# A macaron decoder trunk on one core: seven-product groups put in a set order

## The chip, the core and the metric

The kernel runs on one core of a Trainium2 chip, in one launch. The metric is the device time of that launch in microseconds (us); the program on the core has five engines: TensorE (PE, matmuls), VectorE (DVE), ScalarE (ACT), GpSimd (POOL) and SyncE (SP, which issues the loads).

## What is computed

The input is x (512 tokens, width 1024) and a conditioning vector c. Two layers; each has three sub-layers, with shift, scale and gate made from c:

```python
cs = jax.nn.silu(c)
for l in range(DEPTH):                                   # 2
    mod = (cs @ ada_w[l] + ada_b[l]).reshape(B, N_SUB, 3, D_MODEL)[:, :, :, None, :]
    h = _rmsnorm(x, norm_g[l, 0]) * (1.0 + mod[:, 0, 1]) + mod[:, 0, 0]
    x = x + 0.5 * mod[:, 0, 2] * _swiglu(h, ffn_w_gate[l, 0], ffn_w_up[l, 0], ffn_w_down[l, 0])
    h = _rmsnorm(x, norm_g[l, 1]) * (1.0 + mod[:, 1, 1]) + mod[:, 1, 0]
    x = x + mod[:, 1, 2] * _mixer(h, w_in[l], conv_w[l], w_conv_out[l], w_attn_out[l], w_o[l], rel_bias)
    h = _rmsnorm(x, norm_g[l, 2]) * (1.0 + mod[:, 2, 1]) + mod[:, 2, 0]
    x = x + 0.5 * mod[:, 2, 2] * _swiglu(h, ffn_w_gate[l, 1], ffn_w_up[l, 1], ffn_w_down[l, 1])
return _rmsnorm(x, final_g)
# _swiglu(h, wg, wu, wd) = (silu(h @ wg) * (h @ wu)) @ wd, hidden width 2816
```

The change touches only the gate and up products of `_swiglu`, of which there are four in the program.

## The kernel before

All is float32. Activations stand transposed: `hh` and `hl` hold the sub-layer's input h as a high part (rounded to the matmul's input form) and a low part (the rest), 8 chunks of 128 rows by 512 tokens. Each weight tile is split in the same way: ScalarE casts the high part, VectorE subtracts it for the low part. A product is then three matmuls: high by high, high by low, low by high. Weights are loaded by SyncE into four buffers `raw` of 1 MB; split parts stand in slots of 512 columns, 49 in `R`; float32 scratch in 19 slots `F`. There are eight PSUM banks in three rotations: `mm` (4), `at` (2), `o` (2).

**A feed-forward** (`ffn`, L618) has 22 hidden tiles of 128 rows. The first two (three in the first feed-forward of the program) get their gate and up sums in the stage ahead, `boundary`, and are handed over as `first`, standing in PSUM banks; in the first feed-forward tile 3 is made plainly (16 chunk steps of three matmuls for gate and up). All others are made in pairs by a scheme with seven block products in place of eight (`seven`, L537). With gate weights a (first four chunks) and c (last four), up weights b and d, and h cut in quarters, a pair of tiles needs

- product 1: a by the first chunks of the first half of the tokens, and product 2: c by the last chunks of that half. They need no sum.
- product 5: (b - a) by sum 1; product 6: (d - (b - a)) by sum 2; product 7: (d - b) by sum 3; product 3: d by sum 4. Each needs a block sum of h.
- product 4: (c - (d - b + a)) by the last chunks of the second half.

A product (`product`, L518) is 24 matmuls of 256 columns; it needs a cast of 128x1024 on ScalarE and a low part of 128x1024 on VectorE. Differences of weights are made by VectorE in place in `raw` (L558). Results gather in three banks: `one` (in `mm`, products 1, 6, 7, 4, with copies by ScalarE between them, L554), `two` (in `at`, product 2) and `three` (in `o`, products 5 and 3). VectorE adds the copies and banks (`plus`, L561). `swiglu_pair` then takes the silu of the gates, multiplies, and splits the result into the slots that `down` reads.

**Order.** `ffn` begins with `Sums` (L488): all four block sums of h (VectorE, 128x1024 each, in the float32 copy `whole`, 8 slots of `F`) and their splits, into the upper 16 slots of `R`; `whole` is given back at once. Then the hidden tiles come in five parts (L44: 0 to 6, 6 to 12, 12 to 16, 16 to 19, 19 to 22), most followed by `down`, which multiplies that part's activations with the down weights and adds to x. Within `up` (L664) a group runs 5, 6, 2, 7, then product 1 of the next group (`begin`), then 4, 3, and then its `swiglu_pair`. The text's order is a priority: a planner lays out each engine's instructions from it ahead of time, and may take a later one first where it expects the earlier one not to be ready. On the chip each engine follows the laid-out order.

**Beside it** run, in the first feed-forward and the mixers, modulation steps (L297: load 512 KB of ada weights, multiply and sum on VectorE, 1024 columns). `tick` (L152), called twice a product and every second plain step, lets so many of them through as rate and share allow.

`boundary` (L452) ends the stage before: the last three chunks of its down product, the norm, the modulated h, and the first hidden tiles' sums, in two halves of 256 tokens.

## Time and profile before

| | us |
|---|---|
| median of 3 runs | 2684.92 (2683.99 to 2691.61) |
| the profiled execution | 2685.69 |
| its span on the core | 2683.9 |
| TensorE busy | 2620.5 |
| VectorE busy | 1838.3 |
| ScalarE busy | 1171.6 |

The four feed-forwards start, in the profiled execution, at about 67, 1034, 1391 and 2341 us; between them lie the start of the program (0 to 67), the first mixer (390 to 1010) and the second (1719 to 2318). A matmul counts as busy from its start to the modelled end of its pipeline, so matmuls of 256 columns 0.12 us apart show 0.28 us each. Where a row merges several instructions, x24 is their count. "idle" or a figure in brackets is the time in which the engine did nothing before that instruction, with what ended it.

### The profile page before, as it was taken

How to read it: one execution, taken by the hardware profiler on the slowest of the kernel's cores; microseconds unless marked ns; L12 is line 12 of the kernel's file. 1: busy time of each engine (PE TensorE's matmuls, PEld its weight loads, DVE VectorE, ACT ScalarE, POOL GpSimd, SP SyncE). 2: the span in 40 equal slices, each digit the busy share in tenths (PEclk: the TensorE clock that was granted, in tenths of full speed). 3: DMA queues.
4: the chain of work that ended last, by engine and by line, in shares of the span. 5: the costliest groups of instructions: out<-in, count | busy, mean ns of one | idle time of the engine just before them, and what ended most of it. 6: DMA issues, size and time to landing. Idle time of an engine off the chain costs nothing.

```text
span 2683.9 us, 40526 instructions
## 1 busy us (share of the span) xinstructions
PE 2620.5 (98%) x16265; PEld 2347.2 (87%) x16265; DVE 1838.3 (68%) x2874; ACT 1171.6 (44%) x2200; POOL 227.7 (8%) x551
## 2 busy tenths in 40 slices
PE   6899999999999999999999999999999999999999
PEld 5798999788888889989999999988888888989998
DVE  7996778888463358667787777885536534677675
ACT  4453454343353236434554444543443423544443
POOL 1000023121010001000020000330110000200001
PEclk8999999999999999999999999999999999999999
DMA  8732246767222231333224332562322322133321
GB/s 282 249 128 91 93 146 222 270 203 248 75 95 79 87 118 44 99 110 109 96 64 130 106 110 77 179 217 86 97 69 79 118 81 85 63 111 99 98 83 67
DMA packets 285480, 326.42 MB, mean 122 GB/s; under 512 B 8057, under 2 KB 263404, under 8 KB 285292
## 3 DMA queue, kind: packets, MB, share of 16 engines
q1 hardware_dynamic: 284836, 323.19, 36.8%
q8 instruction: 127, 2.08, 0.3%
q10 hardware_dynamic: 456, 0.65, 0.1%
q14 instruction: 61, 0.50, 0.1%
HBM read 321.67 MB, written 2.13 MB: 121 GB/s over the span
## 4 chain that ended last, share of the span: by engine, by line
PE 84%; DVE 9%; DMA 3%; ACT 3%; issue 1%; POOL 1%; DVEq 0%; POOLq 0%; SPq 0%; ACTq 0%
PE mm L531 16%; PE mm L234 12%; PE mm L235 12%; PE mm L236 12%; PE o L531 8%; PE at L531 4%; PE mm L1046 3%; DMA slots_f<-in_ada_t_dram 2%; DVE slots_f L297 2%; PE o L234 2%; PE o L236 2%; PE o L235 2%; PE at L236 2%; PE at L234 2%; PE at L235 2%; DVE slots_r L145 2%
## 5 line engine op out<-in xcount | busy, mean ns | idle before, releaser
L214 DVE TENSOR_TENSOR slots_r<-raw,slots_r 128x512 fp32r<-128x512 f32 (+2 forms) x578 | 361.0, 642 | 340.5 <-PE mm L235 162.1
L213 ACT CAST slots_r<-raw 128x512 fp32r<-128x512 f32 (+2 forms) x584 | 325.1, 582 | 403.2 <-PE mm L236 170.9
L234 PE MATMUL mm<-hh,slots_r 128*128 128x512 f32 (+1 forms) x1320 | 487.8, 370 | 0.0
L235 PE MATMUL mm<-hl,slots_r 128*128 128x512 f32 (+1 forms) x1320 | 483.0, 366 | 0.0
L236 PE MATMUL mm<-hh,slots_r 128*128 128x512 f32 (+1 forms) x1320 | 482.2, 365 | 0.0
L145 DVE TENSOR_TENSOR slots_r<-raw,slots_r 128x1024 fp32r<-128x1024 f32 (+3 forms) x401 | 379.9, 970 | 130.2 <-ACT slots_r L522 55.4
L522 ACT CAST slots_r<-raw 128x1024 fp32r<-128x1024 f32 x273 | 282.5, 1048 | 363.0 <-DVE raw L558 93.7
L236 PEld LDWEIGHTS mm<-hh,slots_r 128*128 128x128 f32 x1320 | 248.4, 188 | 43.3
L234 PEld LDWEIGHTS mm<-hh,slots_r 128*128 128x128 f32 x1320 | 248.9, 189 | 36.5
L235 PEld LDWEIGHTS mm<-hl,slots_r 128*128 128x128 f32 x1320 | 248.9, 189 | 36.1
L531 PE MATMUL mm<-slots_r 128*128 128x256 f32 x1872 | 240.6, 284 | 3.5 <-ACT slots_r L522 2.2
L531 PE MATMUL o<-slots_r 128*128 128x256 f32 x1872 | 236.3, 283 | 5.1 <-DVE slots_r L145 5.0
L531 PEld LDWEIGHTS o<-slots_r 128*128 128x128 f32 x1872 | 229.9, 191 | 8.1 <-DVE slots_r L145 6.2
L531 PEld LDWEIGHTS mm<-slots_r 128*128 128x128 f32 x1872 | 230.8, 191 | 6.4 <-ACT slots_r L522 2.8
L531 PE MATMUL mm<-hh,slots_r 128*128 128x256 f32 x1248 | 229.5, 280 | 2.7 <-DVE slots_r L145 1.3
L234 PE MATMUL mm<-slots_r 128*128 128x512 f32 (+1 forms) x584 | 212.3, 364 | 0.2 <-ACT slots_r L649 0.2
L235 PE MATMUL mm<-slots_r 128*128 128x512 f32 (+1 forms) x584 | 212.3, 364 | 0.0
L236 PE MATMUL mm<-slots_r 128*128 128x512 f32 (+1 forms) x584 | 212.1, 363 | 0.0
L297 DVE CUSTOM_DVE_ANT_0 slots_f<-slots_f 128x1024 f32<-128x1024 f32 x144 | 176.1, 1232 | 42.0 <-DMA slots_f<-in_ada_t_dram 41.0
L531 PEld LDWEIGHTS mm<-hh,slots_r 128*128 128x128 f32 x1248 | 193.7, 188 | 5.7 <-DVE slots_r L145 2.2
L558 DVE TENSOR_TENSOR raw<-raw 128x1024 f32<-128x1024 f32 x156 | 189.6, 1220 | 2.2
L531 PE MATMUL mm<-hl,slots_r 128*128 128x256 f32 x624 | 174.0, 279 | 0.0
(194 smaller groups left out, 4373.7 us busy)
## 6 DMA issues: line engine op xcount, KB each, us to landing
slots_f<-in_ada_t_dram SPq DMA_DIRECT2D x144, 512.0 KB, 4.5
raw<-in_w_in_dram SPq DMA_DIRECT2D x52, 1024.0 KB, 5.7
raw<-in_ffn_w_gate_dram SPq DMA_DIRECT2D x42, 1024.0 KB, 5.3
raw<-in_ffn_w_up_dram SPq DMA_DIRECT2D x42, 1024.0 KB, 6.2
raw<-in_ffn_w_down_dram SPq DMA_DIRECT2D x32, 768.0 KB, 4.3
raw<-in_w_in_dram SPq DMA_DIRECT2D x48, 512.0 KB, 5.3
raw<-in_ffn_w_down_dram SPq DMA_DIRECT2D x20, 512.0 KB, 3.5
raw<-in_w_conv_out_dram SPq DMA_DIRECT2D x8, 1024.0 KB, 4.8
```

Of the source, the lines that this page charges most:

```text
L145: V.tensor_tensor(out_, a, b, op=ALU.subtract)
L213: A.copy(hv, src)
L214: (eng or V).tensor_tensor(lv, src, f(hv), op=ALU.subtract)
L234: T.matmul(dst, hi, xh[:, cols], start=first, stop=False)
L235: T.matmul(dst, hi, xl[:, cols], start=False, stop=False)
L236: T.matmul(dst, lo, xh[:, cols], start=False, stop=last)
L297: V.tensor_tensor_reduce(out=w, in0=w, in1=cs.ap, scale=1.0, scalar=0.0, op0=ALU.mult, op1=ALU.add, accum_out=m[:, k:k + 1])
L522: A.copy(hv, src)
L531: T.matmul(dst, a, b, start=first and k == i == n == 0, stop=True, skip_group_check=True)
L558: V.tensor_tensor(dst, x, y, op=ALU.subtract)
L1046: T.matmul(dst, a, b, start=k == 0 and r % 2 == 0 and n == 0, stop=True, skip_group_check=True)
```

## The change

- `Sums` no longer makes all sums at once: `make(i)` makes and splits one, and is called from the first group's run: sums 1 and 2 about product 6, sum 3 ahead of product 7, sum 4 ahead of products 4 and 3. `whole` is given back after the first group.
- `product` and `seven` become classes whose splitting and running are separate calls.
- The first group (`first_group`) splits products 1, 2 and 5 ahead of everything else in `ffn`, product 5 into the place of sum 4 (`room`); its loads are asked for there. It keeps its bank `one` in `o` instead of `mm`.
- Ahead of the parts come the swiglus of `first` (odd count) and the plain tile, then products 1 and 2 of the first group.
- A group in `up` runs 5, 6, then 1 of the next group, 7, then 2 of the next group, then 4, 3. Splits 5 and 6 stand first; `swiglu_pair` of the group before stands behind them, or at the end of the part.
- After the last group `R.top` is raised, so that later takers may use all of `R`.

```diff
     class Sums:
+        def make(self, i, whole):
             h11, h21 = whole[:, :4, HALF[0]], whole[:, :4, HALF[1]]
             h12, h22 = whole[:, 4:, HALF[0]], whole[:, 4:, HALF[1]]
-            V.tensor_tensor(h22, h21, h22, op=ALU.add)
-            self.split(0, h22)
-            V.tensor_tensor(h21, h11, h21, op=ALU.subtract)
-            V.tensor_tensor(h22, h22, h11, op=ALU.subtract)
-            self.split(1, h22)
-            self.split(2, h21)
-            V.tensor_tensor(h22, h12, h22, op=ALU.subtract)
-            self.split(3, h22)
+            dst, a, b, op = ((h22, h21, h22, ALU.add), (h22, h22, h11, ALU.subtract),
+                             (h21, h11, h21, ALU.subtract), (h22, h12, h22, ALU.subtract))[i - 1]
+            V.tensor_tensor(dst, a, b, op=op)
+            hi, lo = (v[:, i - 1] for v in self.parts)
+            A.copy(hi, dst)
+            sub(lo, dst, f(hi))
+        def room(self):
+            return [v[:, 3].rearrange("p k n -> p (k n)") for v in self.parts]
...
+    class Seven:
+        def __init__(self, raw1, raw2, sums, tag="mm"):
+            self.a, self.c = raw1[:, :4], raw1[:, 4:]
+            self.b, self.d = raw2[:, :4], raw2[:, 4:]
+            self.sums = sums
+            self.one, self.two, self.three = bank(tag), bank("at"), None
...
+        def run1(self):
+            self.p1.run()
+            self.c11 = self.kept(self.one)
+        def run2(self):
+            self.p2.run()
+            self.plus(self.c11, self.two)
+        def split5(self, room=None):
+            self.minus(self.a, self.b, self.a)
+            self.three = bank("o")
+            self.p5 = Product(self.a, self.sums(1), self.three, True, room)
+        def split6(self):
+            self.minus(self.a, self.d, self.a)
+            self.p6 = Product(self.a, self.sums(2), self.one)
+        def run56(self):
+            self.p5.run()
+            self.p6.run()
+            self.c12 = self.kept(self.one)
...
+        def run43(self):
+            self.p4.run()
+            self.p3.run()
+            self.plus(self.c12, self.three)
+    def first_group(raws):
+        sums = Sums()
+        group = Seven(*raws, sums, "o")
+        group.split1()
+        group.split2()
+        group.split5(sums.room())
+        return group
...
     def ffn(l, i, get, first, whole):
         acts = {}
         R.top = N_LOW
-        sums = Sums(whole.ap.rearrange("p (k n) -> p k n", k=NC))
-        whole.give()
+        group = first_group(get.raws(len(first) + len(first) % 2))
...
+        modulating["share"] = SHARE_UP
+        if len(first) % 2:
+            for n, banks in enumerate(first):
+                swiglu(n, *banks)
+            banks = [any_bank() for _ in range(2)]
+            for pd, u in zip(banks, get(len(first))):
+                project([(pd, u)], h, NC)
+            swiglu(len(first), *banks)
+        group.run1()
+        group.run2()
...
         def up(part):
             modulating["share"] = SHARE_UP
+            late = None
             for m in range(*part):
-                if m in acts:
+                if m not in groups:
                     continue
...
-                pair = ahead.pop(m)
-                next(pair)
-                begin(m + 2)
-                for _ in pair:
-                    pass
-                if m + 2 == DFF // P:
+                here, after = groups.pop(m), None
+                if not begun[0]:
+                    make(1)
+                    here.split6()
+                    make(2)
+                    if len(first) % 2 == 0:
+                        for n, banks in enumerate(first):
+                            swiglu(n, *banks)
+                else:
+                    here.split5()
+                    here.split6()
+                    if late:
+                        swiglu_pair(*late)
+                if m + 2 < DFF // P:
+                    after = groups[m + 2] = Seven(*get.raws(m + 2), sums)
+                    after.split1()
+                here.run56()
+                make(3)
+                here.split7()
+                if after:
+                    after.run1()
+                    after.split2()
+                here.run7()
+                here.split43()
+                make(4)
+                if after:
+                    after.run2()
+                here.run43()
+                if not begun[0]:
+                    begun[0] = True
+                    whole.give()
+                late = m, *here.out()
+                if not after:
                     sums.give()
+                    R.top = N_R
+            if late:
+                swiglu_pair(*late)
```

## Rows read from the trace of the kernel before

**Rows 1.** Busy time of TensorE on the page: us, share of span, instructions
```profile
PE 2620.5 (98%) x16265; PEld 2347.2 (87%) x16265; DVE 1838.3 (68%) x2874; ACT 1171.6 (44%) x2200; POOL 227.7 (8%) x551
```

**Rows 2.** Stretches: busy us and (instructions) of PE, PEld, DVE, ACT, POOL; clock; DMA; GB/s
```profile
390.00:1034.00 644.00, 631.23 (x3425) 540.76 (x3424) 420.36 (x780) 263.23 (x604) 96.24 (x243) 1.00 0.44 146
1034.00:1075.00 41.00, 36.68 (x300) 35.48 (x299) 35.86 (x37) 24.50 (x33) 0.00 (x0) 1.00 0.22 71
...
1391.00:1402.00 11.00, 8.76 (x69) 8.15 (x68) 10.86 (x13) 7.98 (x11) 0.00 (x0) 1.00 0.00 0
1402.00:1719.00 317.00, 317.00 (x2243) 298.15 (x2242) 233.64 (x307) 146.87 (x230) 11.84 (x18) 1.00 0.36 114
...
2341.00:2366.00 25.00, 20.47 (x152) 19.43 (x151) 21.21 (x22) 15.02 (x19) 0.00 (x0) 0.93 0.26 84
...
2352.00:2357.00 5.00, 4.62 (x26) 4.62 (x27) 4.91 (x5) 0.33 (x1) 0.00 (x0) 0.66 0.02 5
```

**Rows 3.** TensorE's waits at A, B, C, D: releaser, us in all, times, longest
```profile
PE at L236 <- DVE slots_r L214: 6.8, 1, 6.8
...
PE o L531 <- DVE slots_r L145: 3.3, 1, 3.3
...
PE mm L531 <- ACT slots_f L627: 1.1, 1, 1.1
...
PE mm L531 <- ACT slots_r L522: 1.7, 1, 1.7
```

**Rows 4.** TensorE in order of time (start, us), and one product from the chain
```profile
68.30 0.39 PE L234 MATMUL mm<-hh,slots_r 128*128 128x512 f32 x1
...
111.28 0.40 PE L234 MATMUL mm<-slots_r 128*128 128x512 f32 x1
...
1034.40 0.39 PE L531 MATMUL o<-slots_r 128*128 128x256 f32 x1
...
1040.20 0.28 PE L531 MATMUL at<-hh,slots_r 128*128 128x256 f32 x1
1043.75 2.90 PE L531 MATMUL o<-slots_r 128*128 128x256 f32 x22 [3.28 <-DVE slots_r L145]
...
1316.62 2.88 PE mm L531 x24
```

**Rows 5.** VectorE in order of time: start, us, what it made, wait ahead of it
```profile
64.50 2.29 DVE L1282 TENSOR_TENSOR slots_f<-hh,hl 128x2048 f32<-128x2048 f32 x1
...
80.46 0.69 DVE L214 TENSOR_TENSOR slots_r<-raw,slots_r 128x512 fp32r<-128x512 f32 x1
...
105.07 1.22 DVE L145 TENSOR_TENSOR slots_r<-raw,slots_r 128x1024 fp32r<-128x1024 f32 x1
...
1023.45 1.23 DVE L495 TENSOR_TENSOR slots_f<-slots_f 128x1024 f32<-128x1024 f32 x1
...
1028.65 2.36 DVE L145 TENSOR_TENSOR slots_r<-raw,slots_r 128x1024 fp32r<-128x1024 f32 x2 [2.71 <-ACT slots_r L522]
...
1042.48 1.22 DVE L145 TENSOR_TENSOR slots_r<-raw,slots_r 128x1024 fp32r<-128x1024 f32 x1
...
1061.43 1.22 DVE L145 TENSOR_TENSOR slots_r<-raw,slots_r 128x1024 fp32r<-128x1024 f32 x1
1062.57 0.68 DVE L561 TENSOR_TENSOR slots_f<-slots_f,o 128x512 f32<-128x512 f32 x1
...
2330.91 1.22 DVE L495 TENSOR_TENSOR slots_f<-slots_f 128x1024 f32<-128x1024 f32 x1
```

**Rows 6.** Groups by line and shape, 67 to 112; the cast from 1023 to 1075
```profile
L297 DVE CUSTOM_DVE_ANT_0 slots_f<-slots_f 128x1024 f32<-128x1024 f32 x9 | 10.9, 1216 | 0.0
...
L145 DVE TENSOR_TENSOR slots_r<-slots_f,slots_r 128x512 fp32r<-128x512 f32 x4 | 2.7, 686 | 0.6 <-ACT slots_r L630 0.6
L561 DVE TENSOR_TENSOR slots_f<-slots_f,o 128x512 f32<-128x512 f32 x2 | 1.4, 688 | 0.2 <-PE o L531 0.2
...
L522 ACT CAST slots_r<-raw 128x1024 fp32r<-128x1024 f32 x15 | 15.2, 1048 | 10.4 <-DVE raw L558 6.5 <-PE o L531 2.1 <-PE mm L531 1.2
```

More of the change, by code (lines that the diff above doesn't have):

```diff
@@ L537, in seven, with __init__, run @@
-    def seven(raw1, raw2, sums, done):
-        a, c = raw1[:, :4], raw1[:, 4:]
-        b, d = raw2[:, :4], raw2[:, 4:]
-        def run(*args):
-            p = product(*args)
-            next(p)
-            return p
-        def end(p):
-            for _ in p:
-                pass
-        def kept(src):
+    class Product:
+        def __init__(self, src, x, bank_, first=False, room=None):
+            self.x, self.bank, self.first = x, bank_, first
+            self.slots = [] if room else [R.take(2), R.take(2)]
+            self.parts = [a.rearrange("p (k m) -> p k m", k=4) for a in room or (s.ap for s in self.slots)]
+            hv, lv = self.parts
+            A.copy(hv, src)
+            sub(lv, src, f(hv))
+        def run(self):
+            hv, lv = self.parts
+            for k in range(4):
+                xh, xl = self.x(k)
+                for i in range(2):
+                    c_ = slice(i * P, (i + 1) * P)
+                    dst = self.bank[:, HALF[i]]
+                    for n, (a, b) in enumerate(((hv[:, k, c_], xh), (hv[:, k, c_], xl), (lv[:, k, c_], xh))):
+                        T.matmul(dst, a, b, start=self.first and k == i == n == 0, stop=True, skip_group_check=True)
+                if k % 2:
+                    tick()
+            for s in self.slots:
+                s.give()
@@ L572, in seven, with split1 @@
-        end(run(a, sums(2), one))
-        u2 = kept(one)
-        two = bank("at")
-        end(run(c, quarter(1, 0), two, True))
-        plus(p1, two)
-        minus(b, d, b)
-        end(run(b, sums(3), one))
-        u3 = kept(one)
-        plus(u3, three)
-        yield
-        minus(c, c, a)
-        end(run(c, quarter(1, 1), one))
-        end(run(d, sums(4), three))
-        plus(u2, three)
-        done(p1, u2, one, u3)
+        def split1(self):
+            self.p1 = Product(self.a, quarter(0, 0), self.one, True)
@@ new lines, in ffn @@
+        wv = whole.ap.rearrange("p (k n) -> p k n", k=NC)
+        sums = group.sums
+        modulating["share"] = SHARE_UP
[8 more added lines that the diff above has]
+        group.run2()
+        groups = {len(first) + len(first) % 2: group}
```

114 lines of the change are left out of this document (43 added, 71 removed).

## The prediction

> **What bounds the kernel now.** I read the page's busy shares first: TensorE is busy 98% of the span [rows 1]. So time can only come from TensorE's own stops or from its clock, as the change removes no matmul. Next the busy time by stretch [rows 2], cut at the four feed-forward starts (I call them A, B, C, D). Between 1402 and 1719, the rest of C with its nine later groups, TensorE is never idle: in the steady run of groups there is nothing to win. All that this change can reach lies just behind the boundaries: 74 to 82 (A), 1034 to 1075 (B), 1391 to 1402 (C), 2341 to 2366 (D). The waits of TensorE there [rows 3] say who ended the stops: a low part from VectorE, a high part or a drained bank from ScalarE. There are 1, 3, 3 and 5 such stops (of each stretch one row stands). Last, the order on the two engines around them [rows 4, 5]: in B the product on bank `o` (product 5) waits 3.28 us for its low part, made at 1042.48, while VectorE, busy 35.9 of the 41 us of B [rows 2], worked on block sums and on the first SwiGLUs. In A the low part of a plain unit comes at 80.46, behind all four sums. So the stops are made by order where VectorE has room, and by its load where it has none. Which is it, for each start?
>
> **VectorE's load up to the last product of the first group.** With the change TensorE runs 1, 2, 5, 6, 1', 7, 2', 4, 3 (a dash marks the next group): nine products at 2.88 us [rows 4]. Before product 3 can start, VectorE must make nine low parts, four raw differences, four sums and four low parts of sums: 21 operations of 128x1024. Two of them back to back take 2.36 us where one takes 1.22 [rows 5, 6], so one each 1.14 us: 23.9 us. Two plus operations and the multiply and low part of each swiglu of the `first` list come on top, at 0.69 us [rows 6].
> B, C and D (no modulations, two swiglus): 23.9 + 6 x 0.69 = 28.0 us. In B VectorE is free at 1023.45 and waits 2.71 us for a slot that the boundary still reads [rows 5]; it would be done at 1023.45 + 2.7 + 28.0 = 1054.2. TensorE, leaving the boundary at 1034.4, comes to product 3 at 1034.4 + 8 x 2.88 = 1057.4 [rows 4]. Slack 3.2 us: order alone can remove these stops. In D VectorE is free at 2330.91 [rows 5] and TensorE at about 2341: 2361.6 against 2364.0, slack 2.4 us. For C I take the same.
> A is different: four swiglus, two plain-unit splits and the modulation steps of its ticks are queued too. The check is the trace itself: VectorE is free at 66.8 (64.50 + 2.29) and ends the last low part of the first group at 106.29 [rows 5], seven modulation steps of 1.2 us among it (nine take 10.9 [rows 6]). The change asks for the same plus one low part (2'), so 107.4; product 3 would end at 107.4 + 2.88 = 110.3. Before, eight products ended at 111.28 [rows 4] and the ninth (2 of the next group) was still to come: 114.2 on the same footing. Gain 3.9 us, not the 6.8 us of the stop. If the planner let every modulation go behind, TensorE would set the end: 68.30 + 48 x 0.23 + 9 x 2.88 = 105.3, gain 8.9; if more modulations came ahead, nothing.
>
> **The change part by part.**
> - Sums at their products, room for product 5 in the fourth sum's place, splits 1, 2 and 5 first: no operation more or less, only order. Takes away in B 41.0 - 36.7 = 4.3 us of idle, in C 11.0 - 8.8 = 2.2, in D 25.0 - 20.5 = 4.5 [rows 2]. The cover is TensorE's own products 1 and 2, which need no sum: 5.8 us in which VectorE makes four operations (4.6 us).
> - Clock: after D's stops 26 matmuls ran between 2352 and 2357 at a mean granted clock of 0.66, part of it at 1.2 GHz, part at 2.4; they took 4.6 us where 26 x 0.12 = 3.1 us is what they take at 2.4 GHz [rows 2]. Gone with the stops: 1.5 us. (In A the clock fell as well, but there VectorE sets the end.)
> - Restart: the 3.28 us stop of B lies between matmul starts 3.55 us apart, against 0.12 within a product: 3.43 lost, 0.15 more than the row says [rows 4]. Eleven stops in B, C and D: 1.7 us.
> - Product 2 a group ahead: one product more per feed-forward runs before the first `down`, one less behind it; within the steady run it is exchanged for product 1', between 6 and 7. The bank `one` is still copied out behind another product each time (1' covers the copy after 6, 2' that after 7). Cost nothing as long as VectorE and ScalarE keep ahead (1402 to 1719: VectorE 234 of 317 us, ScalarE 147 [rows 2]); uncovered it is a copy a group, the third rival's kind of price.
> - Swiglu behind the next splits: its multiplies and low parts (4 x 0.69 on VectorE) move behind two splits; at a part's end it stands ahead of `down` as it did. Who waits: `down` reads the last two activations only at the end of its first jobs, as before. Nothing.
> - Loads: weights of the next group are asked for earlier in the text, past no other load, but the four raw buffers come free by the same last splits of the group before, so the two SyncE issues leave when they did. The eight slots of the whole h are given back later, and the modulation loads of A queue for what is left; bound 0 to one late step (1.2 us), taken 0.
> - New wait: the first group's `one` now stands in a bank `o`, as `three` does, and there are two. Product 5 of the second group, directly behind product 3, needs one of them: it waits for the plus that reads `three` (0.69 us and the drain of the last matmul, 0.28) unless `one` was read by then. Behind it on TensorE stand 6' and all else. In A `down` comes between. Three times 0 to 0.97; I take 0.9, nearest to the plus's own row [rows 6]: 2.7 us lost. Between these two groups the trace of before has no such wait, as `one` was in one of four banks `mm`. The Trainium skill (Perfetto Trace Analysis, Optimization Strategy) says that the same gap coming back can mean that there is not enough PSUM for the next tile; by that rule it would come back at each group, but from the second group on `one` is in `mm` again, so I charge it once a feed-forward.
> - The free slots after the last group (`R.top` raised) change which slots the boundary takes; it can make C like B and D, whose sums share slots with the boundary's units: inside C's slack. Taken as 0, bounds -1 to +1.
>
> Sum: 3.9 + 4.3 + 2.2 + 4.5 + 1.5 + 1.7 - 2.7 = 15.4 us. The profiled execution took 2685.69 us (span 2683.9, 1.8 around it); the median of the three is 2684.92, 0.77 less. 2685.7 - 15.4 - 0.8 = 2669.5 us.
>
> **Rivals.**
> 1. The load, not the order (2684 us). If the slots of the sums are read by the boundary's matmuls to its end, VectorE can begin only at about 1034.4 + 2.3 (a cast and a low part): 1036.7 + 28.0 = 1064.7 against TensorE's 1057.4, so some 7 us of stops, no less than now. It decides from a start 3.2 us later than I assumed. Then B, C and D win nothing and A's 3.9 pays for the banks: -1.2 us. For it: the 2.71 us that VectorE waited there. Against it: behind that wait it made the low parts of two products at 1028.65, well ahead of the boundary's end [rows 5].
> 2. The border of groups (2693 us, slower). Plus of `three` waits for product 3; if the next group's differences and low parts are queued behind it, TensorE stands for 0.69 + 1.22 + 1.05 + 1.22 = 4.2 us (the 1.05 is the cast on ScalarE [rows 6]). There are 23 borders inside the parts; from 0.67 us each on average it eats the whole gain, and every fourth border at 4.2 us costs 24 us. For it: the text of the change puts splits 5 and 6 behind run43, and the steady run has no other cover there. Against: before, the text stood the same way and the trace has the next low part (1061.43) ahead of the plus (1062.57) [rows 5]: the planner put first what was ready first. The Trainium skill (TensorE: Matmul & The Clock Gate, Architectural detail) says that VectorE and ScalarE take their instructions strictly in order, and matmuls stay in program order; by that rule nothing on the chip mends a bad order at a border, and the 80.46 row, a ready split that was late, agrees.
> 3. The change does not do what it says (2685 us). The order on the engines is the planner's; in B the sum-free products already run first. If it keeps its order, nothing changes.
>
> **How the numbers follow.** Forecast 0.60, rival 1 0.20, rival 2 0.15, rival 3 0.05. About 0.3% (8 us) is what a measurement of this kernel can tell from no change: faster below 2677, slower above 2693. Faster 0.60 (the forecast), same 0.24 (rivals 1 and 3 without a remnant), slower 0.16. The low end: A's 8.9 in place of 3.9, no bank waits (2.7) make 2661.8; the rest of the kernel is planned anew too, and its stops (first mixer, 12.8 us between 390 and 1034 [rows 2]) may move by half: 2655. The high end takes in rivals 1 and 3 and the lighter half of rival 2: 2691. Left out are the heavier half of rival 2 and a gain beyond all counted stops.
>
> **What would show it.** Right: no wait of TensorE over 1 us behind the boundary in B and D, and the granted clock at 1.00 there; the first low parts on VectorE are those of 1, 2 and 5, with the sums behind; in A stops of some 5 us are left, late in the group, ended by VectorE; one wait of under 1 us ahead of product 5 of the second group. Wrong: idle of TensorE at borders, ended by VectorE's plus or ScalarE's cast, or a stretch like 1402 to 1719 with idle in it; or A gaining nothing, which would mean that VectorE's load there is larger than counted.

## The result, and the profile after

The changed kernel takes 2674.38 us (median of 5 runs, 2671.10 to 2678.67). The kernel before, run beside it, has the median 2684.92 (5 runs, 2683.99 to 2691.61). The ratio of the two, formed from the runs beside each other, is 0.9948 with a 95% interval of 0.9935 to 0.9960: faster by 0.5%. The forecast was 2669.5 us. The profiled execution of the changed kernel took 2671.10 us (span 2669.3) against 2685.69 (2683.9) before: 14.6 us less, where the sum said 15.4. That single execution is the fastest of its five, so the agreement of these two numbers is closer than what the medians show (10.5 us apart); it is the split of the 14.6 that teaches something, and it isn't the split that was forecast.

The page of the changed kernel, the line that answers to [rows 1]:

```profile
PE 2617.5 (98%) x16265; PEld 2346.9 (88%) x16265; DVE 1832.5 (69%) x2874; ACT 1171.1 (44%) x2200; POOL 232.9 (9%) x551
```

The same instructions on every engine, so only order has changed. The stretches, with the columns of [rows 2] (length, busy us and instructions of PE, PEld, DVE, ACT, POOL; granted clock; DMA share; GB/s):

```profile
390.00:1031.00 641.00, 629.23 (x3404) 540.14 (x3403) 423.45 (x780) 263.42 (x604) 95.80 (x239) 0.99 0.45 147
1031.00:1076.00 45.00, 45.00 (x381) 45.00 (x380) 41.49 (x48) 29.31 (x42) 0.00 (x0) 1.00 0.31 100
1388.00:1402.00 14.00, 14.00 (x118) 13.92 (x118) 13.96 (x15) 6.59 (x10) 0.00 (x0) 1.00 0.23 77
1402.00:1709.00 307.00, 303.96 (x2121) 283.58 (x2120) 218.84 (x294) 139.24 (x219) 9.09 (x14) 1.00 0.35 114
2334.00:2366.00 32.00, 32.00 (x271) 32.00 (x270) 30.84 (x33) 18.08 (x24) 0.00 (x0) 1.00 0.22 69
67.00:112.00 45.00, 42.56 (x284) 38.55 (x283) 44.37 (x59) 23.66 (x36) 0.00 (x0) 1.00 0.65 229
```

Behind the boundaries B, C and D (lines two, three and five) TensorE has no idle time at all, at the full clock, where before it stood 4.3, 2.2 and 4.5 us. Line four is the other side: the rest of C, which had not a moment of idle before, has 3.0 us of it now. The last line is A: TensorE stands 2.4 us of 45, and VectorE is busy 44.4 of the 45.

TensorE's waits, one group of lines for each of two stretches (releaser, us in all, times, longest): 67 to 112, then 1402 to 1700. They answer to [rows 3]; between 1031 and 1076, 1388 and 1402, 2333 and 2640 there are none.

```profile
PE o L538 <- ACT slots_r L501: 1.5, 2, 1.3
PE o L538 <- ACT slots_f L556: 0.4, 1, 0.4
PE o L538 <- DVE slots_r L145: 0.3, 1, 0.3
PE mm L538 <- DVE slots_r L145: 0.3, 1, 0.3
...
PE mm L538 <- ACT slots_f L556: 2.5, 3, 1.2
PE mm L234 <- ACT slots_r L683: 0.5, 1, 0.5
```

(Lines have moved: a product's matmuls are L538 now, were L531; the sums L499, their casts on ScalarE L501; the copies out of a bank L556; the casts of weights L527; the plus L563.) In A the 6.8 us stop is gone, and most of what is left (1.5 of 2.5 us) waits for the cast of a block sum. In C three products waited for a copy out of their bank.

How the time divides is read from TensorE's matmuls. Cut at the first norm matmul of each boundary (386.5, 1000.9, 1358.2, 1709.7, 2308.3 and 2664.3 before; 384.4, 998.2, 1348.2, 1701.5, 2301.5 and 2650.0 after), the stages differ, after minus before, by A -2.1, first mixer -0.6, B -7.3, C +1.7, second mixer +1.4, D -7.5 us. Inside the stages I add up what the starts of neighbouring matmuls lie further apart than their size asks for (0.12 us for 256 columns, 0.235 for 512), in the first 45 us or so of each feed-forward and in its rest:

| lost by TensorE, us (start / rest) | A | B | C | D | mixers |
|---|---|---|---|---|---|
| before | 9.6 / 1.3 | 5.9 / 3.9 | 3.4 / 0.4 | 7.5 / 0.9 | 22.0 + 7.9 |
| after | 4.0 / 4.5 | 0.0 / 2.0 | 0.1 / 5.4 | 0.0 / 0.9 | 22.3 + 8.5 |

The starts won 22.3 us (26.4 to 4.1), the steady run behind them lost 6.3 (6.5 to 12.8), the mixers 0.9: 15.1 us in all, against the 14.6 of the span. So the order at the starts is worth more than the 15.4 us forecast, and a part of it is given back where the forecast saw nothing to lose: the rests lose 3.2 us more in A and 5.0 more in C, 1.9 less in B, and the same in D.

### The profile page after: what moved, and what is told of

It reads as the page before. It is cut to its first block, busy times and chain, and to the rows that moved or that the text cites. A ratio compares the mean times of both kernels' runs of the same rounds, so it can differ in the third digit from the quotient of the medians.

```text
span 2669.3 us, 40518 instructions
## 1 busy us (share of the span) xinstructions
PE 2617.5 (98%) x16265; PEld 2346.9 (88%) x16265; DVE 1832.5 (69%) x2874; ACT 1171.1 (44%) x2200; POOL 232.9 (9%) x551
## 4 chain that ended last, share of the span: by engine, by line
PE 82%; DVE 9%; DMA 4%; ACT 2%; POOL 1%; issue 1%; DVEq 0%; POOLq 0%; SPq 0%; ACTq 0%
PE mm L538 13%; PE mm L234 12%; PE mm L235 12%; PE mm L236 12%; PE o L538 9%; PE at L538 4%; PE mm L1108 3%; DVE slots_f L297 2%; PE o L236 2%; PE o L234 2%; PE o L235 2%; DMA slots_f<-in_ada_t_dram 2%; DVE slots_r L145 2%; PE at L236 2%; PE at L234 2%; PE at L235 2%
## 5 line engine op out<-in xcount | busy, mean ns | idle before, releaser
L527 ACT CAST slots_r<-raw 128x1024 fp32r<-128x1024 f32 x273 | 282.0, 1048 | 334.2 <-DVE raw L560 84.7
L236 PEld LDWEIGHTS mm<-hh,slots_r 128*128 128x128 f32 x1320 | 248.7, 188 | 43.2
L234 PEld LDWEIGHTS mm<-hh,slots_r 128*128 128x128 f32 x1320 | 249.1, 189 | 36.8
L538 PE MATMUL o<-slots_r 128*128 128x256 f32 x2064 | 260.5, 283 | 1.9 <-ACT slots_r L501 1.5
L538 PEld LDWEIGHTS o<-slots_r 128*128 128x128 f32 x2064 | 253.3, 191 | 4.2 <-ACT slots_r L501 1.9
L538 PE MATMUL mm<-slots_r 128*128 128x256 f32 x1680 | 215.5, 284 | 0.7 <-ACT slots_f L556 0.7
L538 PE MATMUL mm<-hh,slots_r 128*128 128x256 f32 x1120 | 211.0, 280 | 2.3 <-ACT slots_f L556 2.0
L538 PEld LDWEIGHTS mm<-slots_r 128*128 128x128 f32 x1680 | 206.9, 191 | 3.1 <-ACT slots_f L556 2.7
L538 PEld LDWEIGHTS mm<-hh,slots_r 128*128 128x128 f32 x1120 | 176.2, 188 | 4.5 <-ACT slots_f L556 3.9
L538 PE MATMUL mm<-hl,slots_r 128*128 128x256 f32 x560 | 156.3, 279 | 0.0
```

Source lines behind the costliest of these rows:

```text
L234: T.matmul(dst, hi, xh[:, cols], start=first, stop=False)
L236: T.matmul(dst, lo, xh[:, cols], start=False, stop=last)
L527: A.copy(hv, src)
L538: T.matmul(dst, a, b, start=self.first and k == i == n == 0, stop=True, skip_group_check=True)
```

## The experiments

Two theories were tested. **Order at the starts**: what VectorE does first behind a boundary makes the whole gain, and the new order of products (2 a group ahead, swiglu late) is what costs in the steady run. Against it: the order of products is needed for the gain, or A's load and the pool of slots carry it. Each run's ratio is to the kernel before, run beside it; that stood at 2691.26, 2691.78 and 2692.32 us in the three batches (e1 to e4, e5 to e8, e9 to e12; each batch ran on a chip of its own). e6 starts from the kernel before and stands in its section.

| run | us, median (range) | ratio, 95% | start / rest: A | B | C | D | mixers |
|---|---|---|---|---|---|---|---|
| e1_first_only | 2667.17 (2665.40 to 2672.45) | 0.9915, 0.9898 to 0.9931 | 6.1 / 3.3 | 1.1 / 0.3 | 1.2 / 0.9 | 1.8 / 2.6 | 16.1 + 11.7 |
| e2_two_at_home | 2678.11 (2677.87 to 2680.50) | 0.9955, 0.9940 to 0.9970 | 6.4 / 8.5 | 1.8 / 2.1 | 1.8 / 0.5 | 1.4 / 1.3 | 23.1 + 9.0 |
| e3_act_at_once | 2675.06 (2674.82 to 2677.52) | 0.9944, 0.9929 to 0.9958 | 6.2 / 3.6 | 0.0 / 4.5 | 0.1 / 1.2 | 0.0 / 1.3 | 25.3 + 10.2 |
| e4_sums_first | 2675.65 (2674.20 to 2680.46) | 0.9947, 0.9932 to 0.9962 | 9.3 / 7.5 | 0.0 / 0.6 | 0.0 / 2.5 | 1.0 / 0.4 | 21.3 + 10.9 |
| e5_mods_later | 2676.20 (2675.31 to 2679.39) | 0.9949, 0.9934 to 0.9963 | 2.0 / 6.8 | 0.0 / 2.7 | 0.1 / 6.4 | 0.0 / 1.2 | 17.0 + 12.9 |
| e7_no_top | 2672.88 (2668.67 to 2680.48) | 0.9937, 0.9919 to 0.9956 | 4.7 / 4.2 | 0.0 / 1.7 | 0.1 / 3.0 | 0.0 / 0.8 | 21.6 + 11.6 |
| e8_tag_mm | 2681.25 (2678.72 to 2684.71) | 0.9965, 0.9952 to 0.9977 | 3.5 / 3.3 | 0.5 / 2.7 | 0.1 / 5.8 | 0.7 / 0.6 | 25.8 + 11.9 |
| e9_two_kept_at_part_end | 2687.90 (2685.90 to 2691.87) | 0.9985, 0.9973 to 0.9996 | 7.1 / 6.1 | 2.1 / 8.7 | 1.0 / 1.2 | 3.3 / 3.8 | 22.8 + 10.6 |
| e10_two_kept_act_at_once | 2681.25 (2676.47 to 2683.59) | 0.9956, 0.9942 to 0.9970 | 6.6 / 3.8 | 0.0 / 0.9 | 0.6 / 5.3 | 1.4 / 3.4 | 27.8 + 9.5 |
| e11_change_again | 2678.02 (2674.72 to 2679.77) | 0.9945, 0.9923 to 0.9966 | 3.9 / 4.1 | 0.0 / 2.7 | 0.1 / 5.6 | 0.0 / 0.7 | 21.7 + 9.6 |
| e12_old_order | 2676.13 (2675.17 to 2681.47) | 0.9943, 0.9921 to 0.9966 | 7.7 / 3.4 | 0.6 / 3.0 | 1.3 / 1.0 | 0.3 / 0.9 | 22.4 + 11.8 |

A warning for reading it: the mixers' code is the same in every kernel, and their sum still goes from 27.8 to 37.7 us, while the same kernel measured twice (the change and e11) has 30.8 and 31.3. I put this down to the planner, which lays out the whole program anew for each text. Two medians less than some 5 us apart can differ by that alone; the stages where an edit acts are what to compare.

### e12_old_order: VectorE's order alone

Products keep the order of the kernel before in all groups (1; 5, 6, 2, 7, the next group's 1, 4, 3), and swiglu follows its group at once. What is left of the change is that the first group's sums are made one by one, behind the splits that need none (with its bank `o`, its room for product 5, its early loads and the raised top).

```diff
         group.split1()
-        group.split2()
         group.split5(sums.room())
...
         group.run1()
-        group.run2()
...
-                    if late:
-                        swiglu_pair(*late)
+                here.run56()
+                make(3)
                 if m + 2 < DFF // P:
                     after = groups[m + 2] = Seven(*get.raws(m + 2), sums)
+                here.split2()
+                here.run2()
+                here.split7()
+                here.run7()
+                if after:
                     after.split1()
-                here.run56()
-                make(3)
-                here.split7()
-                if after:
                     after.run1()
-                    after.split2()
-                here.run7()
                 here.split43()
                 make(4)
-                if after:
-                    after.run2()
                 here.run43()
...
-                late = m, *here.out()
+                swiglu_pair(m, *here.out())
...
```

> The products in the order of the kernel before throughout (1, then 5, 6, 2, 7, 1', 4, 3, swiglu behind its group); only the first group's work on VectorE and ScalarE is put right: splits of 1 and 5 ahead of all, each sum at its product. Theory (the order on VectorE is what made the starts stop; which product runs first on TensorE matters little): B, C and D start with under 2 us of stops each, total some 15 to 24 us below the kernel before, as in the run with the first group alone. Rival (products 1 and 2 are needed ahead as cover while sum 1 is made): product 5 waits 2 us or more in B and D for the low part of sum 1 or of its split, 5 us or more slower than the run with the first group alone (0.9915 of the kernel before).

2676.13 us, ratio 0.9943: the change itself, run beside it as e11, has 0.9945. At B, C and D there is next to nothing left to win (stretches 1031 to 1076 and 2334 to 2366, then TensorE's only wait between 1030 and 1075):

```profile
1031.00:1076.00 45.00, 44.75 (x376) 44.51 (x375) 37.12 (x42) 24.53 (x35) 0.00 (x0) 1.00 0.27 84
2334.00:2366.00 32.00, 32.00 (x269) 31.77 (x268) 30.48 (x33) 21.78 (x28) 0.00 (x0) 1.00 0.22 67
...
PE o L538 <- DVE slots_r L145: 0.2, 1, 0.2
```

Where before product 5 waited 3.28 us for its low part in B, here it waits 0.2, and no product has moved. The new order of products gives 2 us more at the starts of B, C and D (2.2 us of stops in all against 0.1), 3.7 us more in A and 1.0 in the rest of B, and loses 4.4 in the rest of C and 1.1 in that of A: over the whole kernel, nothing that shows, with intervals of some 6 us to either side. The rival's wait of 2 us in B and D did not come. Its price did: against the kernel before, e12 is 7.5 us slower than e1 (0.9943 and 0.9915, with intervals that overlap). By the table 6.4 us of that lie in the mixers, and the starts and rests of the two differ by 0.9 us in all.

### e4_sums_first: do the sums have to wait?

The reverse: products in the order of the change, but all four sums ahead of products 5 to 3 (product 5 with slots of its own).

```diff
-        group.split5(sums.room())
+        group.split5()
+        for i in (1, 2, 3, 4):
+            sums.make(i, wv)
...
         def make(i):
-            if not begun[0]:
-                sums.make(i, wv)
+            pass
```

> As the changed kernel, but all four block sums are made and split at once, right behind the splits of products 1, 2 and 5 and ahead of the first swiglus; product 5 then has slots of its own. Theory (VectorE has some 3 us of slack up to product 3 in B, C and D, so the place of the sums matters little once the splits of 1, 2 and 5 are ahead; in A its load sets the end either way): B and D keep at least two thirds of their gain, total within 4 us of the changed kernel. Rival (the place of each sum at its product is what removes the stops): stops of 2 to 5 us come back in B and D, 6 to 12 us slower than the changed kernel.

2675.65 us, ratio 0.9947. B, C and D start nearly as smoothly as in the change (0.0, 0.0, 1.0 us of stops), so there the sums' own place doesn't matter once the splits of products 1, 2 and 5 stand ahead of them, and neither does the room in the fourth sum's place. In A it does. TensorE's wait of 67 to 112, then a row of ScalarE and two of VectorE in order of time (start, us):

```profile
PE o L538 <- DVE slots_f L666: 7.3, 1, 7.3
...
68.16 0.61 ACT L665 ACTIVATE slots_f<-o 128x512 f32<-128x512 f32 x1
...
79.35 1.21 DVE L499 TENSOR_TENSOR slots_f<-slots_f 128x1024 f32<-128x1024 f32 x1
80.48 0.67 DVE L666 TENSOR_TENSOR slots_f<-slots_f,o 128x512 f32<-128x512 f32 x1
```

L666 is the multiply of a swiglu of `first`. The activation that it reads was written by ScalarE at 68.8 (68.16 + 0.61); the multiply ran at 80.48, behind the fourth sum, VectorE without a pause between, and bank `o`, which it frees, held product 5 for 7.3 us. That is the 80.46 row of [rows 5] with another operation in it: a ready operation late in its engine's order. The Trainium skill (TensorE: Matmul & The Clock Gate, Architectural detail) says that ScalarE and VectorE are strictly first in, first out; this row agrees.

### e5_mods_later and e6_before_mods_later: is A the load?

In both the modulation steps that tick along with the matmuls are put off, and the forced ones stand behind the first `down` matmuls: in e5, on the changed kernel, until the first group of a feed-forward is over; in e6, on the kernel before, over its whole first part (the share there is `SHARE_UP if part[0] else 0.0`). The diff is that of e5.

```diff
             raw = load(src[:, 2 * j * P:(2 * j + 2) * P])
+            jobs = [(any_bank(), u) for u in halves_of(raw, kc)]
+            project(jobs, rhs, kc)
             if j == 0:
                 while sub_layer not in ready:
                     next(modulating["gen"])
             gate = mods[sub_layer]
-            jobs = [(any_bank(), u) for u in halves_of(raw, kc)]
-            project(jobs, rhs, kc)
...
-        modulating["share"] = SHARE_UP
+        modulating["share"] = 0.0
...
-            modulating["share"] = SHARE_UP
+            modulating["share"] = SHARE_UP if begun[0] else 0.0
```

> The changed kernel with one edit in the first feed-forward (A): no modulation step is let through until its first group is done; they are made up for in the first down, where the forced ones now come behind the first job's matmuls. All steps are still done. Theory (VectorE's load, some seven steps of 1.2 us among it, sets the end of A's first group): the stops of TensorE between 67 and 112, 4.0 us in the trace of the changed kernel, fall under 1.5 us; the steps return behind 112, so the feed-forward as a whole gains 0 to 4 us. Rival (order again: a wrong place of sums 2 and 4 makes these stops): 3 us or more of them stay.

> The same edit on the kernel before: in the first feed-forward no modulation step until the first part's groups are done. Theory: A's stop of 6.8 us was made by the four sums queued ahead of a plain unit's split, with one modulation step among them, so it falls by 1 to 2 us only, to 5 or 6. Rival (the modulation load alone made it): under 2 us.

TensorE's waits between 67 and 112, of e5 and then of e6:

```profile
PE mm L236 <- DVE slots_r L214: 1.1, 1, 1.1
```

```profile
PE at L236 <- DVE slots_r L214: 5.7, 1, 5.7
```

With the order right, taking the load away ends the stops on sums: in e5 only an order stop is left (the split of a plain unit), and the 421st matmul starts at 102.7 us, against 105.5 in the change and 110.9 before. The start still loses 2.0 us, where under 1.5 were expected. With the order wrong, the load hardly matters: e6 still waits 5.7 us of 6.8, as expected, and takes 2696.68 us (2691.91 to 2701.42), ratio 1.0020 (1.0010 to 1.0029): no faster, if anything slower. But e5 ends A at 384.6 us and the change at 384.4: the steps that were put off come back behind the first group, where the rest of A loses 6.8 us instead of 4.5.

### e3_act_at_once and e2_two_at_home: what stops the steady run?

e3 puts swiglu back to the end of its group; e2 puts product 2 back into its own group, from the second group on.

```diff
-                    if late:
-                        swiglu_pair(*late)
...
-                late = m, *here.out()
+                swiglu_pair(m, *here.out())
...
-            if late:
-                swiglu_pair(*late)
```

```diff
+                here.run56()
+                make(3)
...
+                if begun[0]:
+                    here.split2()
+                    here.run2()
+                else:
                     after.split1()
-                here.run56()
-                make(3)
                 here.split7()
-                if after:
+                if after and not begun[0]:
                     after.run1()
-                    after.split2()
                 here.run7()
+                if after and begun[0]:
+                    after.split1()
+                    after.run1()
                 here.split43()
                 make(4)
-                if after:
-                    after.run2()
```

> As the changed kernel, but each group's swiglu stands right behind the group, ahead of the next group's splits. Theory (where the swiglu stands does not matter while VectorE and ScalarE keep ahead of TensorE): within 3 us of the changed kernel, C's stops still there. Rival (the swiglu ahead of splits 5 and 6 delays them at a border): stops of 0.7 us or more ahead of product 5 at the borders, up to 23 times, 5 to 16 us slower than the changed kernel.

> As the changed kernel, but product 2 runs in its own group (5, 6, 2, 7, then 1', 4, 3); the swiglu stays behind the next group's splits. Theory (running 1' and 2' ahead uses up the products that cover the copies of the bank after a down, and leaves 6, 7, 4 back to back): no stop of 0.8 us ended by the copy of the bank in C, 3 to 7 us less than the changed kernel. Rival (the copies come late because the swiglu and the splits stand ahead of them on ScalarE): the same stops in C as in the changed kernel, time within 2 us of it.

First what they are to explain, in the changed kernel itself. TensorE and then ScalarE, in order of time, in the first group of C behind a `down`:

```profile
1469.16 2.88 PE L538 MATMUL mm<-slots_r 128*128 128x256 f32 x22
1472.72 3.14 PE L538 MATMUL mm<-slots_r 128*128 128x256 f32 x24 [0.68 <-ACT slots_f L556]
1476.53 0.38 PE L538 MATMUL mm<-hh,slots_r 128*128 128x256 f32 x1 [0.68 <-ACT slots_f L556]
```

```profile
1472.08 0.58 ACT L556 COPY slots_f<-mm 128x512 f32<-128x512 f32 x1 [0.45 <-PE mm L538]
...
1475.89 0.58 ACT L556 COPY slots_f<-mm 128x512 f32<-128x512 f32 x1 [2.28 <-PE mm L538]
```

Products 6, 7 and 4 run back to back on one bank, and each must wait for the copy of what the one before left there: 0.83 us from start to start more than within a product. The products that were to cover the copies, 1 and 2 of the next group, had run already: their matmuls stand ahead of and among those of product 5, between 1460.05 and 1469, probably because the splits of 5 and 6 came late (that is read from the order of the rows and not tested). A third stop of this kind is at the last group (1.33 us at 1669), which has no next group to borrow from.

Both edits took these stops away: 1.2 and 0.5 us are left in the rest of C. The waits between 1402 and 1700 are, for e3 (at the last group) and then e2 (at 1408, still in the first group, so it counts with the start's 1.8 us),

```profile
PE mm L538 <- ACT slots_f L556: 0.5, 1, 0.5
```

```profile
PE o L538 <- ACT slots_f L556: 1.3, 1, 1.3
```

So the expectation for e3, that C's stops stay, was wrong, though its time was right; that for e2 was right on these stops of C and wrong on the total. Neither kernel is faster than the change: e3 loses 4.5 us in the rest of B, where the last group now waits 1.8 us for a copy, and e2 8.5 in the rest of A. An uncovered copy can stand with either half of the change taken out, as the plan falls.

### e1_first_only: both at once

The edits of e2 and e3 together: the change's first group, and the old order of products and swiglu from the second group on.

> Only the first group of each feed-forward is handled as in the change (splits 1, 2, 5 ahead, each sum at its product); later groups run 5, 6, 2, 7, 1', 4, 3 as before, with the swiglu right behind its group. Theory (the gain is made at the four starts, the steady run has nothing to win and the change loses some there): the starts in B, C and D without a stop of over 1 us, C's later stops (some 7.6 us in the trace of the changed kernel behind 1402, against 1.8 before) gone, so 4 to 8 us less than the changed kernel, about 2664 to 2668 beside its 2671 to 2674. Rival (the order of the steady run is part of the gain): slower than the changed kernel by 3 us or more.

2667.17 us, ratio 0.9915 (0.9898 to 0.9931): the fastest kernel of the study, 0.8% under before, and its interval lies clear of that of the change as first measured (0.9935 to 0.9960; that of e11, on another chip, is wider and reaches down to 0.9923). The starts keep 1.1, 1.2 and 1.8 us of stops, in D one of 1.3 us where none over 1 us was expected, and the steady run behind them is near what it was (3.3, 0.3, 0.9, 2.6).

Where its lead over the change comes from is not shown. By the table it loses 6.0 us less than e11 in the rests, 6.2 us more at the starts, and 3.5 us less in the mixers, which no edit reaches. The first mixer alone is 5.9 us shorter than before (608.5 against 614.4 us between the marks), as its stop near 481 us is 1.4 us here and 4.7 before, and the second is 3.6 us longer. That the edit brings this is not shown; it came with this plan.

### e9_two_kept_at_part_end and e10_two_kept_act_at_once: a cure that isn't one

Here the next group's product 2 is kept for its own group at the border to a `down`, so that a covering product is at hand there; e10 has swiglu at once as well.

```diff
...
+                own = here.p2 is None
                 here.run56()
                 make(3)
+                if own:
+                    here.split2()
+                    here.run2()
                 here.split7()
-                if after:
+                if after and not own:
                     after.run1()
-                    after.split2()
+                    if m + 2 < part[1]:
+                        after.split2()
                 here.run7()
+                if after and own:
+                    after.run1()
+                    if m + 2 < part[1]:
+                        after.split2()
...
-                if after:
+                if after and m + 2 < part[1]:
                     after.run2()
```

> The changed kernel, but product 2 is not run ahead across the end of a part: the last group of a part leaves it to its own group, which runs 5, 6, 2, 7, 1', 4, (2') 3. So each group behind a down, and the program's last group, has a product between 6 and 7 again. Theory (C's later stops come from groups whose 1' and 2' are used up, so that the copies of the bank between 6, 7 and 4 are uncovered): stops behind the starts fall from 12.8 us in the trace of the changed kernel to under 7, the starts stay at 4 to 5 us, time 4 to 8 us below the changed kernel run beside it. Rival (those stops are accidents of each plan): they move to other places, the sum behind the starts stays at 10 us or more.

> The run above with each swiglu right behind its group, as in the kernel before. Theory: within 3 us of the run above, as the place of the swiglu did not matter in the steady run. Rival: stops at the borders, 4 us or more slower.

2687.90 and 2681.25 us, against 2678.02 for the change run beside them (e11). In e9 C's rest is down to 1.2 us, as meant, but B's is up to 8.7. Its waits of TensorE between 1076 and 1360:

```profile
PE mm L538 <- ACT slots_f L557: 3.2, 3, 2.5
PE mm L234 <- ACT slots_r L684: 2.1, 1, 2.1
```

The same kind of stop (L557 is the copy out of the bank), larger, in another stage. The rests lose 19.8 us in all, where the theory said under 7 and the rival 10 or more: the rival's side came out. e10 was to lie within 3 us of e9 and is 6.7 us faster, which neither side of its expectation had. So the reading of C above, true for its place, is no recipe; what covers the copies in one stage can leave them bare in another, and I can't say from these runs what order would cover all.

### e7_no_top and e8_tag_mm: the small parts

```diff
                     sums.give()
-                    R.top = N_R
```

```diff
-        group = Seven(*raws, sums, "o")
+        group = Seven(*raws, sums, "mm")
```

> The changed kernel without raising the upper bound of the slots after the last group (the boundary takes its slots as before). Theory (this part is worth little): every start within 1 us of the changed kernel, total within 4 us. Rival (the slots it frees are what lets C and the mixers start well, or what costs C its later stops): C or the first mixer differs by 3 us or more.

> The changed kernel with one edit: the first group keeps its bank in the rotation of four, as before, not in that of two. Those four hold the first tiles' sums at the start, so product 1 can run only after a first swiglu has read its bank. Theory (bank o is what lets product 1 run first; no wait for it at the border of the first two groups was seen): TensorE stands 1 to 3 us at the start of B, C and D each, ended by the silu of a first tile, 3 to 8 us slower than the changed kernel. Rival (2, then 5 cover it, as they need other banks): within 2 us.

Without the raised top (e7) every start is within 1 us of the change and the time is 2672.88 us, ratio 0.9937: that part is worth nothing that shows. With `one` of the first group in a bank `mm` (e8) the stops that were expected at the starts didn't come (0.5, 0.1, 0.7 us). It is slower than the runs beside it all the same (0.9965), with 25.8 us of stops in the first mixer, and why stays open.

### e11_change_again: order or chance?

The changed kernel once more, on the chip of e9, e10 and e12.

> The changed kernel itself, on this chip, as the mark for the others and to see which of its stops come back: those in C at the second part (two of 0.8 us) and the absence of any at the starts of B, C and D should be the same, as the order is fixed; stretches at a lower clock, some 3 us long, may stand elsewhere. 0.9930 to 0.9960 of the kernel before.

Ratio 0.9945, as the first time, and the stops of C are back at their places. TensorE at 1473:

```profile
1473.60 3.14 PE L538 MATMUL mm<-slots_r 128*128 128x256 f32 x24 [0.68 <-ACT slots_f L556]
```

They belong to the order of the instructions and not to one execution.

## Why the prediction was right, and where it was not

**Order against load, B, C and D: right.** The slack said to be 3.2 and 2.4 us was enough: there is no stop behind a boundary (its size wasn't measured). e12 shows that the order on VectorE and ScalarE does it with the products in their old order, and e4 that the sums need not wait for their products once the splits of 1, 2 and 5 stand ahead (in e12 that of 2 does not). VectorE at B answers to [rows 5]: two sums fill the time in which no slot is free, then three low parts of weights that need no sum come, before TensorE leaves the boundary at 1031.49, and the sums' low parts follow.

```profile
1020.75 2.48 DVE L499 TENSOR_TENSOR slots_f<-slots_f 128x1024 f32<-128x1024 f32 x2
1026.11 3.50 DVE L145 TENSOR_TENSOR slots_r<-raw,slots_r 128x1024 fp32r<-128x1024 f32 x3 [2.88 <-PE mm L236]
1029.52 2.35 DVE L560 TENSOR_TENSOR raw<-raw 128x1024 f32<-128x1024 f32 x2
1031.79 2.35 DVE L145 TENSOR_TENSOR slots_r<-slots_f,slots_r 128x1024 fp32r<-128x1024 f32 x2
```

The size: B and D won 7.3 and 7.5 us, where idle, restarts and D's clock summed to 4.8 and 6.8. In D that is within 1 us. In B it is the stops that the stretch of 41 us cut off or held in pieces too small to list (5.9 us by matmul starts against 4.3 of idle) and 1.9 us of the rest of B, which no term had: the prediction read the steady run off C alone, which lost 0.4 us in its rest, while that of B lost 3.9.

**Rival 1, the load (0.20): no** in B, C and D. VectorE waited 2.88 us for the boundary's slots as before (2.71), and it was not late. It was right for A alone, where it was part of the forecast.

**A: the place right, the size not.** The stops that are left stand late in the group, with VectorE busy 44.4 of 45 us. The longest is ended by a cast on ScalarE, and that had waited for VectorE's sum:

```profile
100.26 1.22 DVE L499 TENSOR_TENSOR slots_f<-slots_f 128x1024 f32<-128x1024 f32 x1
101.40 0.68 DVE L563 TENSOR_TENSOR slots_f<-slots_f,o 128x512 f32<-128x512 f32 x1
```

```profile
102.61 0.38 PE L538 MATMUL o<-slots_r 128*128 128x256 f32 x1 [1.28 <-ACT slots_r L501]
```

The fourth sum ends at 101.48, and TensorE goes on with product 3 when ScalarE has cast it. That leaves 4.0 us of stops (said: some 5). At the end of the group the gain is even larger than the term of 3.9 us: the 421st matmul starts 5.4 us earlier than before (105.5 against 110.9). But it does not last to the end of the stage: the 700th starts 2.9 us earlier, the 1000th 2.1, and the boundary 2.1. The rest of A gives back 3.2 us, some 2 of them at one place, between 117.6 and 120.4, where TensorE waits for the cast of down weights. The chain behind that cast goes back over a load to VectorE (start, us):

```profile
110.81 0.95 DVE slots_r L214 x2
...
111.83 7.01 DMA raw<-in_ffn_w_down_dram
...
118.86 1.46 ACT slots_r L213 x3
```

The load leaves when VectorE's low parts have freed its buffer, at 111.83 here and at 111.33 before, although TensorE is some 5 us ahead. The step that failed is that a gain at the end of the first group is a gain of the stage: VectorE, as loaded behind it as in it (8.0 of 8 us between 112 and 120), takes it back. In e5 TensorE waits in the rest of A for VectorE's low parts themselves (1.4 and 1.3 us).

**New wait for a bank `o`, 2.7 us: nothing.** The lower bound held. Between groups 1 and 2 of B, products 3 and 5 run back to back; ScalarE's read of `one` was early enough:

```profile
1054.28 5.93 PE L538 MATMUL o<-slots_r 128*128 128x256 f32 x48
```

```profile
1055.20 0.59 ACT L676 ACTIVATE slots_f<-o 128x512 f32<-128x512 f32 x1
```

The step put the price of the plus's row on the wait because it was the nearest row; the `unless` in the same sentence (`one` read by then) was the case.

**Product 2 a group ahead and swiglu late, "cost nothing": wrong.** This is the step that failed most. C loses 5.0 us more in its rest than before (5.4 against 0.4), 3.0 of them in three copies that no product covers (0.83, 0.83 and 1.33). The step held that the copies stay behind another product and that uncovered they cost a copy a group ("the third rival's kind of price" there is that of the second). The kind of price was right, the condition wasn't: it asked whether VectorE and ScalarE keep ahead on average, 234 and 147 of 317 us, and they do. What counted in C is one group behind a `down` and the last one, where covering products had been used up early or don't exist; C's other borders, B and D show no such stop. C came out at +1.7 us in place of -1.8. The text itself named this sign ("a stretch like 1402 to 1719 with idle in it"). Swiglu late was taken at nothing too, and in C a matmul of `down` waits 0.5 us for the cast of the last swiglu (the L683 row), in B one 0.7; but e3, with swiglu at once, has such a wait of 0.6 in B, so the late place isn't shown to be the cause.

**Rival 2 (0.15): its kind of cost, a quarter of its size.** 6.3 us of stops came in the rests, 5.0 of them in C, not the 24 of its heavy half, and not at the plus of `three` but at the copies.

**Rival 3 (0.05): no.** The order on VectorE did change, though two of the sums still stand first where they cost nothing.

The errors thus cancel, and that the forecast lies within 5 us of the median is in part luck: the starts won 22.3 us where their terms sum to 18.1, the bank waits of 2.7 didn't come, and 6.3 us of new stops and 0.9 in the mixers were not foreseen. What stays open: which order covers every copy (e2, e3, e9 and e10 each moved the stops), why e8 is slower, and how much of e1's lead is its own. What swiglu's late place costs by itself isn't settled either: with swiglu at once e10 is faster than e9 and e3 stands where the change stands.

## What to carry to other kernels

Put the order of the helping engines at the start of a stage right before the order of the bound engine's own work is touched: here the first gave all of the gain, the second nothing that shows. A product kept to be run ahead is cover for copies that come later, so ask of each border (behind another stage, at the last group) what still covers them there, and not only of the average. And where the helping engine is full, as in A, a better order brings the gain forward and the load takes it back, so cost it at the end of the stage.

## What the runs showed of the hardware

A stop can be followed by a lower clock in one execution and not in another of the same kernel. Four stretches of 2 us around the stop of 0.8 us (by matmul starts; 0.58 idle) at the norm of the boundary to B, of e11 and then two that hold the same stop in the changed kernel's first profile (columns of [rows 2]):

```profile
1006.00:1008.00 2.00, 1.42 (x11) 1.14 (x10) 2.00 (x6) 1.47 (x4) 0.36 (x1) 1.00 0.00 0
1008.00:1010.00 2.00, 2.00 (x15) 2.00 (x16) 0.92 (x4) 1.91 (x4) 1.16 (x2) 0.76 0.03 8
1010.00:1012.00 2.00, 2.00 (x11) 2.00 (x11) 1.31 (x6) 0.60 (x1) 0.87 (x2) 0.50 0.00 0
1012.00:1014.00 2.00, 2.00 (x17) 2.00 (x16) 0.93 (x3) 0.05 (x1) 0.00 (x0) 0.88 0.01 4
```

```profile
1008.00:1010.00 2.00, 1.42 (x13) 1.22 (x12) 1.78 (x6) 1.56 (x5) 0.44 (x1) 1.00 0.00 0
1010.00:1012.00 2.00, 2.00 (x19) 2.00 (x19) 0.89 (x4) 1.27 (x3) 0.93 (x2) 1.00 0.03 8
```

In e11 TensorE, idle for 0.6 of 2 us, ran its next matmuls at the granted clock 0.50, which is 1.2 GHz, before it rose again to 2.4: 11 matmuls in 2 us where 19 ran in the other execution. Stage B took 352.3 us there and 350.0 in the first profile; 0.7 us of that are stops in its rest (2.7 against 2.0). In the kernel before, the 3.28 us stop of B left the clock at 1.00, while the 6.8 us stop of A was followed by 0.50 (80 to 86). So the clock behind a stop is not read off its length here, and runs of one kernel differ by such falls.

And a stop of TensorE costs 0.15 us more than its idle row says: 0.83 us are lost from start to start where the row reads 0.68, 3.43 where it reads 3.28. That lies in how the row counts: the matmul ahead of the stop shows as busy for 0.28 us, while within a product the next one starts 0.12 us after it.
